# Regrouping the rows of a ReLU row sum into three contiguous blocks of 15, 97 and 16 rows per partition, with a final store of 64 B rows

## The chip, the cores and the metric

One core of a Trainium2 chip. Three of its engines matter here: VectorE and ScalarE compute, and SP issues the DMAs, the transfers between the memory of input and output and the core's own buffers. The trace lists each DMA as packets. When a DMA's data are in place, it has raised its semaphore, a counter that an engine can wait for; that moment is called its landing. The metric is the device time of one execution in microseconds (us), lower is better. A run lists its time and the span of the profiled records, which is about 1.5 us shorter.

## The reference

```python
def setup_inputs():
    batch, seq, dim = 32, 512, 1024
    return {"x": np.random.randn(batch, seq, dim).astype(np.float32)}

def reference(x):
    return np.sum(np.maximum(x, 0), axis=-1).astype(np.float32)
```

The input is 16,384 rows of 1024 floats, 4 KB each, 67.1 MB in all. The output is one float per row, 64 KB. With 128 partitions each partition gets 128 rows.

## The kernel before

Seven chunks of 16 rows per partition go through three buffers, and then a tail of 8, 4, 2 and 1 rows and one last row in two halves. In each chunk but the last, ScalarE applies ReLU and VectorE reduces; in four rows of the sixth chunk, in the last chunk and in the tail both engines do ReLU and sum row by row in one instruction. All loads and stores are issued by SP. Which rows a partition owns is free, since rows are independent. Before, the first 2048 rows form a block of their own (16 neighbouring rows per partition, so partition p starts 64 KB after partition p-1), and all others form a block of 112 rows per partition (a pitch of 448 KB). In the output, each partition's results within a block are contiguous too.

```python
    x0 = xr[0 : P * BIG, :].rearrange("(p j) d -> p j d", p=P)      # block 1: 16 rows per partition
    o0 = of[0 : P * BIG].rearrange("(p j) -> p j", p=P)
    xv = xr[P * BIG :, :].rearrange("(p j) d -> p j d", p=P)        # block 2: 112 rows per partition
    ov = of[P * BIG :].rearrange("(p j) -> p j", p=P)
    # ... cut: buffers and semaphores ...
    for c in range(NBIG + 1):                                       # the chunks
        if c >= NB:
            sp.wait_ge(s_dve, 3 * (c - NB + 1))                     # a buffer is free again
        if c < NBIG:
            sp.dma_start(
                out=buf[:, c % NB, :, :],
                in_=xv[:, (c - 1) * BIG : c * BIG, :] if c else x0[:, :, :],
            ).then_inc(s_in[c], 16)
    # ... cut: loads of the tail (8, 4, 2, 1 rows) ...
    sp.dma_start(                                                   # last row, first half
        out=buf[:, tb, r, 0 : LAST[0]], in_=xv[:, J - BIG - 1, 0 : LAST[0]]
    ).then_inc(s_in[-2], 16)
    sp.dma_start(out=last[:, 0 : LAST[1]], in_=xv[:, J - BIG - 1, LAST[0] : D]).then_inc(
        s_in[-1], 16                                                # last row, second half
    )
    sp.dma_start(out=o0[:, :], in_=res[:, 0:BIG]).then_inc(s_out0, 16)   # early store, 64 B rows
    # ... cut: the work on the chunks and the tail ...
    act.wait_ge(s_in[-2], 16)
    on_act(buf[:, tb, BIG - 1, 0 : LAST[0]], last[:, LAST[1] : LAST[1] + 1]).then_inc(s_tact, 1)
    dve.wait_ge(s_tact, 1)
    dve.wait_ge(s_in[-1], 16)
    on_dve(last[:, :], res[:, J - 1 : J]).then_inc(s_tdve, 1)       # 512 values and ScalarE's sum
    sp.wait_ge(s_tdve, 1)
    sp.dma_start(out=ov[:, :], in_=res[:, BIG:J]).then_inc(s_out, 16)    # final store, 448 B rows
    sp.wait_ge(s_out0, 16)
    sp.wait_ge(s_out, 16)
```

## Time and profile before

| | before |
|---|---|
| time, median of the first 3 runs | 162.49 us (162.36 to 162.69) |
| span of the profiled run | 161.0 us |
| DMA: share of 16 engines' span | 97.1% |
| VectorE, ScalarE busy | 76%, 63% |
| a 64 KB packet repeats on an engine every | 2.414 us, or 434 GB/s on 16 engines |

The page of the kernel before: the DMA rows of the slices (tenths of the engines busy, then GB/s), the queue, and the issues to the output (size in KB, us from issue to landing).

```profile
span 161.0 us, 144 instructions
...
DMA  7979979979979979979979979979979969999992
GB/s 260 521 309 472 521 309 472 521 309 472 521 309 472 521 309 472 521 309 472 521 309 472 521 309 472 521 309 472 521 309 472 521 260 521 391 391 431 413 403 71
...
q1 hardware_dynamic: 2160, 67.18, 97.1%
...
out_dram<-res SPq DMA_DIRECT2D x1, 56.0 KB, 1.6
```

The swing between 309 and 521 GB/s is no stall: the 64 KB packets of the 16 engines start within 0.8 us of each other, every 2.414 us, and a slice of 4.03 us sees sometimes more of these starts and sometimes fewer. The queue is busy from its first load to its last, so the loads set the time. What is left lies before the first packet and after the last one.

The head and the end of the kernel before, from its timeline (start us, us, engine, line, operation, and in brackets the idle time before it and what ended it):

```profile
22.77 14.04 ACT L107 ACTIVATE buf<-buf 128x4096 f32<-128x4096 f32 x3 [20.77 <-DMA buf<-in_x_dram]
...
157.96 0.63 ACT L87 ACTIVATE buf<-buf 128x512 f32<-128x512 f32 x1 [0.81 <-DMA buf<-in_x_dram]
158.44 0.08 DVE L90 DVE_READ_ACCUMULATOR buf<-buf 128x1 f32 x1
158.50 0.19 ACT L87 ACTIVATION_READ_ACCUMULATOR buf<-buf 128x1 f32 x1
158.72 0.69 DVE L90 TENSOR_SCALAR_CACHE_REDUCE last<-last 128x513 f32<-128x513 f32 x1 [0.19 <-ACT buf L87]
159.33 0.08 DVE L90 DVE_READ_ACCUMULATOR last<-last 128x1 f32 x1
159.44 0.34 SPq L140 DMA_DIRECT2D out_dram<-res  x1
```

ScalarE's first activation marks when chunk 0 has landed. At the end, the last VectorE instruction waits for ScalarE's half row. The final store is issued at 159.44, and the span ends 1.6 us later.

### The profile page before, as it was taken

The numbers are of one execution on the slowest core, as the hardware profiler recorded it, in microseconds if no ns is written. First come the engines' busy times: TensorE is split into PE (matmuls) and PEld (weight loads), VectorE is DVE, ScalarE is ACT, GpSimd is POOL, SyncE is SP. The second block draws the span as 40 slices with busy tenths as digits, with TensorE's granted clock in tenths as the row PEclk, the third lists the DMA queues.
The fourth block names the chain that finished last, engine by engine and source line by source line (L and its number), as shares of the span: only waits on it lengthen the run. The fifth ranks groups of instructions, "written<-read, shape, count | busy, mean of one in ns | idle before, by whom it ended". The sixth has DMA issues, their size and how long they took to land.

```text
span 161.0 us, 144 instructions
## 1 busy us (share of the span) xinstructions
DVE 122.0 (76%) x56; ACT 101.0 (63%) x55; POOL 0.2 (0%) x4
## 2 busy tenths in 40 slices
DVE  0000004998969898898969989699899999598995
ACT  3000039991599907997099951999339980596972
POOL 0000000000000000000000000000000000000000
DMA  7979979979979979979979979979979969999992
GB/s 260 521 309 472 521 309 472 521 309 472 521 309 472 521 309 472 521 309 472 521 309 472 521 309 472 521 309 472 521 309 472 521 260 521 391 391 431 413 403 71
DMA packets 2160, 67.18 MB, mean 417 GB/s; under 512 B 496, under 2 KB 496, under 8 KB 880
## 3 DMA queue, kind: packets, MB, share of 16 engines
q1 hardware_dynamic: 2160, 67.18, 97.1%
HBM read 67.11 MB, written 0.07 MB: 417 GB/s over the span
## 4 chain that ended last, share of the span: by engine, by line
DMA 69%; ACT 18%; DVE 10%; SPq 1%; issue 0%
DMA buf<-in_x_dram 69%; ACT buf L107 17%; DVE res L109 9%; SPq L71 1%; ACT buf L87 0%; DVE last L90 0%; SPq L64 0%
## 5 line engine op out<-in xcount | busy, mean ns | idle before, releaser
L109 DVE TENSOR_REDUCE res<-buf 128x4 f32<-128x4096 f32 (+3 forms) x18 | 100.4, 5604 | 34.5 <-ACT buf L107 34.5
L107 ACT ACTIVATE buf<-buf 128x4096 f32<-128x4096 f32 (+3 forms) x18 | 80.9, 4555 | 47.3 <-DMA buf<-in_x_dram 47.3
L87 ACT ACTIVATE buf<-buf 128x1024 f32<-128x1024 f32 (+1 forms) x18 | 18.4, 1024 | 9.7 <-DMA buf<-in_x_dram 9.7
L90 DVE TENSOR_SCALAR_CACHE_REDUCE buf<-buf 128x1024 f32<-128x1024 f32 x18 | 21.0, 1216 | 2.7 <-DMA buf<-in_x_dram 2.5
L87 ACT ACTIVATION_READ_ACCUMULATOR buf<-buf 128x1 f32 x18 | 3.4, 189 | 0.0
L107 ACT ACT_TABLE_LOAD x1 | 1.3, 1283 | 0.7 <-PEq L156 0.7
L90 DVE DVE_READ_ACCUMULATOR buf<-buf 128x1 f32 x18 | 1.5, 83 | 0.0
L90 DVE TENSOR_SCALAR_CACHE_REDUCE last<-last 128x513 f32<-128x513 f32 x1 | 0.7, 689 | 0.2 <-ACT buf L87 0.2
L156 POOL MEMSET const-bfloat16-1.0<- 128x1 bf16 x1 | 0.1, 102 | 0.0
L156 POOL MEMSET const-uint8-127<- 128x1 uint8 x1 | 0.1, 102 | 0.0
L156 POOL MEMSET const-float32-0.0<- 128x1 f32 x1 | 0.1, 99 | 0.2 <-issue 0.2
L156 POOL MEMSET const-float32-1.0<- 128x1 f32 x1 | 0.1, 99 | 0.0
L90 DVE DVE_READ_ACCUMULATOR last<-last 128x1 f32 x1 | 0.1, 84 | 0.0
## 6 DMA issues: line engine op xcount, KB each, us to landing
buf<-in_x_dram SPq DMA_DIRECT2D x1, 4096.0 KB, 26.7
buf<-in_x_dram SPq DMA_DIRECT2D x1, 2048.0 KB, 31.2
buf<-in_x_dram SPq DMA_DIRECT2D x1, 1024.0 KB, 33.2
buf<-in_x_dram SPq DMA_DIRECT2D x1, 512.0 KB, 34.0
buf<-in_x_dram SPq DMA_DIRECT2D x1, 256.0 KB, 34.2
last<-in_x_dram SPq DMA_DIRECT2D x1, 256.0 KB, 34.3
buf<-in_x_dram SPq DMA_DIRECT2D x7, 36.3
out_dram<-res SPq DMA_DIRECT2D x1, 56.0 KB, 1.6
```

The costliest lines, as they stand in the source:

```text
L71: sp.dma_start(out=buf[:, tb, r : r + n, :], in_=xv[:, (NBIG - 1) * BIG + r : (NBIG - 1) * BIG + r + n, :],).then_inc(s_in[NBIG + i], 16)
L87: return act.activation(t, t, AF.Relu, accum_out=acc)
L90: return dve.tensor_scalar(out=t, in0=t, scalar1=0.0, scalar2=None, op0=ALU.max, op1=ALU.add, accum_out=acc)
L107: act.activation(t, t, AF.Relu).then_inc(s_act, 1)
L109: dve.tensor_reduce(out=res[:, c * BIG + r : c * BIG + r + n], in_=t, axis=X, op=ALU.add).then_inc(s_dve, 1)
L156: nc = _bacc.Bacc("TRN2", target_bir_lowering=False, num_devices=1)
```

## The change

Its intent is to shorten the end: if the last 16 rows of each partition are a block of their own, the final store writes 16 results per partition (64 B) in place of 112 (448 B), and the others go out earlier, behind the loads. The remaining 112 rows are cut 15 + 97, so the first chunk needs two loads (15 rows of block 1, one row of block 2), and the pitches between partitions become 60, 388 and 64 KB.

```diff
+REGIONS = [15, 97, 16]
+CHUNKS = [[(0, 0, 15), (1, 0, 1)]] + [[(1, 16 * c + 1, 16)] for c in range(6)]
-    x0 = xr[0 : P * BIG, :].rearrange("(p j) d -> p j d", p=P)
-    o0 = of[0 : P * BIG].rearrange("(p j) -> p j", p=P)
-    xv = xr[P * BIG :, :].rearrange("(p j) d -> p j d", p=P)
-    ov = of[P * BIG :].rearrange("(p j) -> p j", p=P)
+    start = [sum(REGIONS[:i]) for i in range(len(REGIONS))]
+    xv = [
+        xr[P * s : P * (s + n), :].rearrange("(p j) d -> p j d", p=P)
+        for s, n in zip(start, REGIONS)
+    ]
+    ov = [of[P * s : P * (s + n)].rearrange("(p j) -> p j", p=P) for s, n in zip(start, REGIONS)]
 ... cut ...
-            sp.dma_start(
-                out=buf[:, c % NB, :, :],
-                in_=xv[:, (c - 1) * BIG : c * BIG, :] if c else x0[:, :, :],
-            ).then_inc(s_in[c], 16)
+            i = 0
+            for g, j, n in CHUNKS[c]:
+                sp.dma_start(
+                    out=buf[:, c % NB, i : i + n, :], in_=xv[g][:, j : j + n, :]
+                ).then_inc(s_in[c], 16)
+                i += n
 ... cut: the tail is read from xv[-1], waits count the loads of a chunk ...
-    sp.dma_start(out=o0[:, :], in_=res[:, 0:BIG]).then_inc(s_out0, 16)
+    sp.wait_ge(s_fact, 1)          # both engines are done with the last chunk
+    sp.wait_ge(s_fdve, 1)
+    for g in range(len(REGIONS) - 1):
+        sp.dma_start(
+            out=ov[g][:, :], in_=res[:, start[g] : start[g] + REGIONS[g]]
+        ).then_inc(s_store, 16)
 ... cut ...
     sp.wait_ge(s_tdve, 1)
-    sp.dma_start(out=ov[:, :], in_=res[:, BIG:J]).then_inc(s_out, 16)
-    sp.wait_ge(s_out0, 16)
+    sp.dma_start(out=ov[-1][:, :], in_=res[:, start[-1] : J]).then_inc(s_out, 16)
+    sp.wait_ge(s_store, 16 * (len(REGIONS) - 1))
     sp.wait_ge(s_out, 16)
```

More of the change, by code (lines that the diff above doesn't have):

```diff
@@ L6 @@
 BIG = 16
-NBIG = 7
 NTWO = 6
 NB = 3
+REGIONS = [15, 97, 16]
+CHUNKS = [[(0, 0, 15), (1, 0, 1)]] + [[(1, 16 * c + 1, 16)] for c in range(6)]
 STEPS = [4, 5, 7]
@@ L33, in bass_relu_sum_kernel @@
     J = B * S // P
-    assert BIG * NBIG + sum(TAIL) + 1 == J and sum(LAST) == D
+    NBIG = len(CHUNKS)
+    assert BIG * NBIG + sum(TAIL) + 1 == J == sum(REGIONS) and sum(LAST) == D
     xr = x.rearrange("b s d -> (b s) d")
     of = out.rearrange("b s -> (b s)")
-    x0 = xr[0 : P * BIG, :].rearrange("(p j) d -> p j d", p=P)
-    o0 = of[0 : P * BIG].rearrange("(p j) -> p j", p=P)
-    xv = xr[P * BIG :, :].rearrange("(p j) d -> p j d", p=P)
-    ov = of[P * BIG :].rearrange("(p j) -> p j", p=P)
+    start = [sum(REGIONS[:i]) for i in range(len(REGIONS))]
[4 more added lines that the diff above has]
+    ov = [of[P * s : P * (s + n)].rearrange("(p j) -> p j", p=P) for s, n in zip(start, REGIONS)]
     buf = nc.alloc_sbuf_tensor("buf", [P, NB, BIG, D], fp32)
@@ L50, in bass_relu_sum_kernel @@
     s_dve = nc.alloc_semaphore("s_dve")
+    s_fact = nc.alloc_semaphore("s_fact")
+    s_fdve = nc.alloc_semaphore("s_fdve")
     s_tact = nc.alloc_semaphore("s_tact")
     s_tdve = nc.alloc_semaphore("s_tdve")
-    s_out0 = nc.alloc_semaphore("s_out0")
+    s_store = nc.alloc_semaphore("s_store")
     s_out = nc.alloc_semaphore("s_out")
@@ L70, in bass_relu_sum_kernel @@
     for i, n in enumerate(TAIL):
-        sp.dma_start(
-            out=buf[:, tb, r : r + n, :],
-            in_=xv[:, (NBIG - 1) * BIG + r : (NBIG - 1) * BIG + r + n, :],
-        ).then_inc(s_in[NBIG + i], 16)
+        sp.dma_start(out=buf[:, tb, r : r + n, :], in_=xv[-1][:, r : r + n, :]).then_inc(
+            s_in[NBIG + i], 16
+        )
         tail.append((r, n, s_in[NBIG + i]))
         r += n
-    sp.dma_start(
-        out=buf[:, tb, r, 0 : LAST[0]], in_=xv[:, J - BIG - 1, 0 : LAST[0]]
-    ).then_inc(s_in[-2], 16)
-    sp.dma_start(out=last[:, 0 : LAST[1]], in_=xv[:, J - BIG - 1, LAST[0] : D]).then_inc(
+    sp.dma_start(out=buf[:, tb, r, 0 : LAST[0]], in_=xv[-1][:, BIG - 1, 0 : LAST[0]]).then_inc(
+        s_in[-2], 16
+    )
+    sp.dma_start(out=last[:, 0 : LAST[1]], in_=xv[-1][:, BIG - 1, LAST[0] : D]).then_inc(
         s_in[-1], 16
     )
-    sp.dma_start(out=o0[:, :], in_=res[:, 0:BIG]).then_inc(s_out0, 16)
+    sp.wait_ge(s_fact, 1)
[4 more added lines that the diff above has]
+        ).then_inc(s_store, 16)
     def on_act(t, acc):
@@ L98, in bass_relu_sum_kernel @@
         b, steps = c % NB, STEPS if c < NTWO - 1 else MIXED
-        act.wait_ge(s_in[c], 16)
+        act.wait_ge(s_in[c], 16 * len(CHUNKS[c]))
         if steps is MIXED:
-            dve.wait_ge(s_in[c], 16)
+            dve.wait_ge(s_in[c], 16 * len(CHUNKS[c]))
             for i in (BIG - 4, BIG - 3):
@@ L119, in bass_relu_sum_kernel @@
     for c in range(NTWO, NBIG):
-        act.wait_ge(s_in[c], 16)
-        dve.wait_ge(s_in[c], 16)
+        act.wait_ge(s_in[c], 16 * len(CHUNKS[c]))
+        dve.wait_ge(s_in[c], 16 * len(CHUNKS[c]))
         for i in range(BIG):
-            (on_act if i % 2 else on_dve)(*row(c, i))
+            ins = (on_act if i % 2 else on_dve)(*row(c, i))
+            if i >= BIG - 2:
+                ins.then_inc(s_fact if i % 2 else s_fdve, 1)
     for r, n, s in tail:
```

## The prediction

> **What bounds the kernel now.** The load stream. The DMA queue view has it busy for 97.1% of 16 engines' span, and the slices show no hole. In the DMA packet records the loads run for 156.4 us (67.1 MB). Each engine starts a 64 KB packet every 2.414 us, so 16 engines move 434 GB/s. The Trainium skill, "DMA: Bandwidth & Descriptors", section Specifications, names a fabric ceiling of 435 GB/s; the trace agrees, so the steady stream has nothing to gain. VectorE is 76% and ScalarE 63% busy, and SP's waits show that buffers come free early: chunk 3 is issued at 44.5 us behind two queued chunks, the tail's loads at 122 us, 16 us before chunk 6 lands. The engines do not hold up the stream.
>
> Outside it lie a head of 2 us (with first packets of 2.9 to 3.6 us) and an end of 2.6 us (timeline): the last load lands at 158.46, the last VectorE work runs 158.72 to 159.42, the final store is issued at 159.44, its packets run 160.6 to 160.97, and the span ends at 161.04. The unprofiled time is 1.4 us more.
>
> **What the change does.**
>
> 1. The final store shrinks from 128 rows of 448 B to 64 B, on the critical path. Its issue and the 1.2 us to its first packet stay. Its packets take 0.336 us from first to last, some 0.1 of it skew between engines; the rest is 8 packets of 25 ns and one for the semaphore per engine. The old 64 B store's packets were 7 ns apart. Estimate: 8 x (25 - 7) = 0.15 us less.
>
> 2. The other results go in two earlier stores (60 B and 388 B rows), issued when chunk 6 is done at 148.2 us. They queue behind the tail's loads, as the old 64 B store did, take some 0.3 us per engine and end over a microsecond before the final store's first packet. Their issues, 0.4 us each, fall in SP's idle wait of 34.2 us. Worth 0.
>
> 3. The first chunk becomes two loads: 8 more packets and a semaphore packet per engine. A 4 KB packet repeats every 155 ns, a 64 KB one every 2.414 us, which fits 4.4 ns per packet plus a fixed rate: 8 x 4.4 + 6 = 0.04 us more, on the path.
>
> 4. The row pitch between partitions goes from 64 KB (first chunk) and 448 KB (the rest) to 60, 388 and 64 KB. Packets already run at the ceiling; I expect the same rate. The head could move by 0.2 us either way, and the tail's short packets (4 KB in 159 ns, 2 KB in 84 to 96 ns) may slow a little at the 64 KB pitch. I book 0.
>
> Sum: -0.15 + 0.04 = -0.1 us, below 0.1%.
>
> **Predicted time:** 162.35 us, range 161.8 to 162.9. Chances: faster by over 2% 0.01, within 2% 0.98, slower by over 2% 0.01.
>
> **What would show it.** Step 1: final store from issue to landing 1.4 to 1.5 us, not 1.6. Step 2: the early stores land before the final one's first packet. Step 3: 128 packets each of 60 KB and 4 KB, chunk 0 landing within 0.1 us of before. Step 4: 64 KB packets still 2.42 to 2.43 us on average; loads 156.4 us from first to last.
>
> **What would make it wrong.** A pitch that makes packets slow or uneven among engines (loads over 157 us); a faster head from the new addresses; unaligned 60 B and 388 B stores so slow that they delay the last load on a late engine or the final store behind them.

## The result, and the profile after

| | before | after |
|---|---|---|
| time, median of 6 runs each | 162.53 us (162.33 to 162.71) | 162.78 us (162.44 to 163.05) |
| ratio | 1 | 1.0015, 95% interval 1.0000 to 1.0029 |
| span of the profiled run | 161.0 us | 161.3 us |

A ratio is the mean time of one kernel's fast runs over the mean of the other's of the same rounds, so it is not quite the ratio of the medians. The change gained nothing; it may have cost 0.25 us. That is far inside 2%, but its sign is not the predicted one, and the later runs confirmed it: a second timing of the changed kernel gave 1.0030 (1.0018 to 1.0042).

The page of the changed kernel, the same rows as above (the three issues to the output are from its DMA view):

```profile
span 161.3 us, 147 instructions
...
DMA  7999999979979979989989989989989989999992
...
q1 hardware_dynamic: 2448, 67.18, 97.1%
...
out_dram<-res SPq DMA_DIRECT2D x1, 48.5 KB, 10.5
out_dram<-res SPq DMA_DIRECT2D x1, 7.5 KB, 10.1
out_dram<-res SPq DMA_DIRECT2D x1, 8.0 KB, 1.4
```

The final store now takes 1.4 us from issue to landing in place of 1.6. The step that the change was made for works.

The head and the end of the changed kernel, from its timeline:

```profile
23.09 14.04 ACT L120 ACTIVATE buf<-buf 128x4096 f32<-128x4096 f32 x3 [21.08 <-DMA buf<-in_x_dram]
...
158.25 0.63 ACT L100 ACTIVATE buf<-buf 128x512 f32<-128x512 f32 x1 [0.80 <-DMA buf<-in_x_dram]
158.75 0.08 DVE L103 DVE_READ_ACCUMULATOR buf<-buf 128x1 f32 x1
158.79 0.19 ACT L100 ACTIVATION_READ_ACCUMULATOR buf<-buf 128x1 f32 x1
159.17 0.69 DVE L103 TENSOR_SCALAR_CACHE_REDUCE last<-last 128x513 f32<-128x513 f32 x1 [0.34 <-DMA last<-in_x_dram]
159.78 0.08 DVE L103 DVE_READ_ACCUMULATOR last<-last 128x1 f32 x1
159.89 0.33 SPq L155 DMA_DIRECT2D out_dram<-res  x1
```

Two things moved. ScalarE's first activation starts 0.32 us later (23.09 against 22.77), and the loads after it keep that delay. And the last VectorE instruction now waits for its own data: ScalarE was done at 158.98, but the second half row came only at 159.05.

The semaphore records of the trace date every landing to the nanosecond. Each load has 16 increments in the trace, and the time of the sixteenth is its landing (chunk 0 of the changed kernel has two loads, so there it is the thirty-second). All values from the span's start, in us:

```
                                   before    after
chunk 0 landed                     22.750   23.064
chunk 6 landed                    138.870  139.185
  from chunk 0 to chunk 6         116.120  116.121
last row, first half landed       157.940  158.229
last row, second half landed      158.574  159.048
  between the halves                0.634    0.819
last load packet ended            158.103  158.401
```

The stream from chunk 0 to chunk 6 takes the same 116.12 us, although its pitch changed from 448 to 388 KB. The loss sits in the first chunk (0.31 us) and between the two halves of the last row (0.19 us). In that last place the data packets are not late: the last load packet ended 0.30 us later than before, which is the head's delay, but its landing came 0.65 us after it and not 0.47 us.

The prediction's times of packets are on another zero than the timeline: they are 0.36 us late. Its "last load lands at 158.46" is the end of the last load packet, 158.10 us here, and its final store's "160.6 to 160.97" is 160.28 to 160.62 us. From issue to first packet the final store took 0.84 us and not 1.2.

### The profile page after: what moved, and what is told of

The parts are those of the page before. It is cut to its first block, busy times and chain, and to the rows that moved or that the text cites. A ratio compares the mean times of both kernels' runs of the same rounds, so it can differ in the third digit from the quotient of the medians.

```text
span 161.3 us, 147 instructions
## 1 busy us (share of the span) xinstructions
DVE 122.0 (76%) x56; ACT 101.0 (63%) x55; POOL 0.2 (0%) x4
## 4 chain that ended last, share of the span: by engine, by line
DMA 69%; ACT 17%; DVE 10%; SPq 2%; issue 0%; DVEq 0%
DMA buf<-in_x_dram 48%; DMA last<-in_x_dram 21%; ACT buf L120 17%; DVE res L122 9%; SPq L80 1%; SPq L73 1%; DVE last L103 0%; SPq L85 0%; DVEq L150 0%
```

## The experiments

Twelve kernels were run, four at a time on one chip, each in 5 rounds beside the kernel before; the four share its runs. Three theories stood at the start:

- Head theory: the changed first chunk makes the head longer, through its split (two loads) or through its pitch of 60 KB.
- Early-store theory: the two early stores, which stand in the queues behind the last loads, delay the landing of the last load.
- Chance theory: head and tail move by 0.3 us from run to run, whatever the kernel.

The head is measured by one more number from the packet records: when the slowest of the 16 engines ends its first packet. The records do not name the engine, but in the first chunk each engine's packets follow each other without a gap, so the sixteen chains can be told apart by their times. Where the first packet is 60 KB and not 64 KB, 0.15 us is added, the time of the missing 4 KB at the steady rate, so that all can be compared.

The table has all traces, in us. "Halves" is the time between the landings of the two halves of the last row; "4 KB packets" is the mean duration of the tail's 4 KB packets in ns.

| kernel | first packets end: mean, slowest | chunk 0 landed | chunk 6 to 1-row load | halves | 4 KB packets | ratio to before (95%) |
|---|---|---|---|---|---|---|
| before | 5.04, 5.49 | 22.75 | 18.41 | 0.634 | 162 | 1 |
| before_again | 5.05, 5.30 | 22.56 | 18.39 | 0.625 | 162 | 0.9999 (0.9987 to 1.0011) |
| after | 5.20, 5.74 | 23.06 | 18.40 | 0.819 | 162 | 1.0015 (1.0000 to 1.0029) |
| after_again | 5.20, 5.62 | 22.95 | 18.38 | 1.202 | 164 | 1.0030 (1.0018 to 1.0042) |
| split_only | 5.02, 5.42 | 22.85 | 18.38 | 0.623 | 162 | 1.0008 (0.9996 to 1.0021) |
| no_split | 5.05, 5.43 | 22.70 | 18.65 | 0.672 | 199 | 1.0003 (0.9989 to 1.0017) |
| no_split_again | 5.11, 5.35 | 22.64 | 18.39 | 0.662 | 179 | 0.9991 (0.9978 to 1.0003) |
| no_early | 5.20, 5.84 | 23.15 | 18.38 | 0.605 | 162 | 1.0027 (1.0015 to 1.0040) |
| split_later | 5.17, 5.71 | 22.96 | 18.40 | 0.931 | 165 | 1.0030 (1.0017 to 1.0042) |
| two_blocks | 5.04, 5.36 | 22.59 | 18.38 | 0.685 | 167 | 1.0000 (0.9986 to 1.0013) |
| pitch_68 | 5.14, 5.83 | 23.05 | 18.39 | 0.632 | 161 | 1.0028 (1.0015 to 1.0040) |
| shift_4k | 4.97, 5.27 | 22.52 | 18.39 | 0.630 | 161 | 1.0003 (0.9990 to 1.0016) |
| swap_stores | 5.05, 5.25 | 22.52 | 18.67 | 0.854 | 191 | 1.0003 (0.9989 to 1.0016) |
| partial_rows | 5.03, 5.29 | 22.57 | 18.47 | 0.679 | 187 | 0.9995 (0.9982 to 1.0007) |

From chunk 0 to chunk 6 all fourteen traces lie between 116.08 and 116.15 us. Each kernel or repeat has one trace, so the columns are read by groups of traces, and the ratios come from all of a kernel's runs.

### before_again: the kernel before, unchanged

> The kernel before, unchanged: a control for noise, in time and in the trace. Every theory: ratio 1.000, within 0.001. Head theory (the changed first chunk makes the head 0.3 us longer): ScalarE's first activation starts within 0.1 us of 22.77 us, as in the first trace of before. Chance theory (head and tail move by 0.3 us from run to run whatever the kernel): it starts elsewhere by 0.2 us or more, towards the 23.09 us of the changed kernel.

Measured: 162.36 us against 162.44 us, ratio 0.9999. The first activation started at 22.58 us, 0.19 us earlier than in the first trace, so the head does move by 0.2 us by itself, which is more than the head theory had allowed. But it moved away from the changed kernel's 23.09 us. Everything after chunk 0 repeated: from the landing of chunk 0 to the last VectorE work it took 135.92 us (135.97 in the first trace), and from there to the span's end 2.32 us both times.

### after_again: the changed kernel, unchanged

> The changed kernel once more. Head theory: ratio to before 1.0015 to 1.002 again, ScalarE's first activation again at 23.0 to 23.2 us, last VectorE work again at about 159.15 us. Chance theory: ratio between 0.999 and 1.001, first activation anywhere from 22.7 to 23.1 us.

Measured: 162.92 us against 162.44 us, ratio 1.0030, above the expected range of the head theory. The first activation came at 22.97 us (just under the expected 23.0). The last VectorE work came at 159.42 us, later than expected, because the halves were now 1.20 us apart. So the loss is no chance, and it has two parts of which the second varies: 0.16 us in one trace, over 0.5 us in the other. The lines of this kernel's last instruction and of its wait, from the view of that tile:

```profile
L103 DVE TENSOR_SCALAR_CACHE_REDUCE last<-last x1: 690/690/690, 159.4 to 159.4; 128x513 f32<-128x513 f32 x1
...
  DMA last<-in_x_dram: 0.7, 1
```

The second line says that the engine sat idle for 0.7 us until the load of `last` had landed.

### no_split: blocks of 16, 96 and 16 rows

```diff
-REGIONS = [15, 97, 16]
-CHUNKS = [[(0, 0, 15), (1, 0, 1)]] + [[(1, 16 * c + 1, 16)] for c in range(6)]
+REGIONS = [16, 96, 16]
+CHUNKS = [[(0, 0, 16)]] + [[(1, 16 * c, 16)] for c in range(6)]
```

> Blocks of 16, 96 and 16 rows per partition, the first chunk one load of 16 rows: the change without its split and without the 60 KB pitch, with its early stores and its 64 B final store. Head theory: first activation back at about 22.77 us, time 0.3 us below the changed kernel, so 0.999 to 1.000 of before. Early-store theory (the two early stores behind the last loads delay the last landing by 0.16 us): only that much stays, so with the 0.2 us saved by the store the ratio is 0.9995 to 1.0. Chance theory: about 0.999, the store's 0.15 to 0.2 us alone.

Measured: 162.56 us against 162.44 us, ratio 1.0003. The first activation went back to 22.72 us, as the head theory has it, and the halves to 0.67 us. From the last VectorE work to the span's end it took 2.17 us, so the final store's gain is in the trace. But it did not show in the time: the tail from chunk 6 to the one-row load took 18.65 us and not 18.40. The miss is told with the second run of this kernel below.

### split_only: the kernel before with its first chunk loaded in two parts

```diff
-            sp.dma_start(
-                out=buf[:, c % NB, :, :],
-                in_=xv[:, (c - 1) * BIG : c * BIG, :] if c else x0[:, :, :],
-            ).then_inc(s_in[c], 16)
+            i = 0
+            for n in (15, 1) if c == 0 else (BIG,):
+                src = xv[:, (c - 1) * BIG : c * BIG, :] if c else x0[:, i : i + n, :]
+                sp.dma_start(out=buf[:, c % NB, i : i + n, :], in_=src).then_inc(s_in[c], 16)
+                i += n
```

(The first wait of ScalarE counts 32 and not 16.)

> The kernel before with only its first chunk split into loads of 15 rows and 1 row, same addresses, pitch 64 KB, same stores. By my sum of packet overheads: 0.04 us longer, ratio 1.0002, first activation at about 22.81 us. Head theory with the split as the cause: 0.3 us longer, ratio 1.002, first activation at about 23.1 us. Head theory with the 60 KB pitch as the cause: as by my sum.

Measured: 162.60 us against 162.44 us, ratio 1.0008, with an interval that holds both 1.0002 and 1.002. The first activation came at 22.87 us, 0.1 us after the first trace of before and 0.29 us after the second. The first packets ended as early as before (mean 5.02, slowest 5.42), unlike in the changed kernel (5.20; 5.74 and 5.62). So the split alone does not make the slow first packets. From the slowest first packet to the chunk's last semaphore packet this trace took 17.09 us against 16.90 before, 0.19 us where my sum has 0.04; in the two traces of the changed kernel it took 16.94 and 16.95, which is my sum (16.95 in no_early, which has the same split). One trace cannot say more than that the split costs between 0.04 and 0.2 us.

### no_early: the changed kernel without its early stores

```diff
-    for g in range(len(REGIONS) - 1):
-        sp.dma_start(
-            out=ov[g][:, :], in_=res[:, start[g] : start[g] + REGIONS[g]]
-        ).then_inc(s_store, 16)
...
-    sp.wait_ge(s_store, 16 * (len(REGIONS) - 1))
```

The output is wrong.

> The changed kernel without its two early stores; their results are missing, so the output is wrong on purpose. Early-store theory (the unaligned 60 B and 388 B rows, queued behind the last loads, delay the last load's landing): the last half row lands 0.62 to 0.68 us after the first half, as before (0.82 and 1.20 us in the two traces of the changed kernel), the last VectorE work is released by ScalarE and no longer by the load, and the time falls 0.2 to 0.5 us below the changed kernel's. If the landing is late for another reason (chance, or the tail's 64 KB pitch): no change in either.

Measured: the halves went back to 0.605 us, and the last VectorE work was again released by ScalarE:

```profile
L99 DVE TENSOR_SCALAR_CACHE_REDUCE last<-last x1: 690/690/690, 159.1 to 159.1; 128x513 f32<-128x513 f32 x1
...
  ACT buf L96: 0.2, 1
```

From the landing of chunk 0 to the last VectorE work it took 135.91 us, as in the kernel before. But the time did not fall: 162.87 us, ratio 1.0027, where 0.2 to 0.5 us less than the changed kernel had been expected. This run's head was the slowest of all (chunk 0 at 23.15 us, one engine's first packet starting only at 3.39 us), and its final store was issued 0.08 us later after the last VectorE work than in the changed kernel. Together these ate what the tail gave back against the first trace of the changed kernel (spans 161.31 and 161.34 us), but not all of it against the second (161.58 us). For the other four executions there is no trace; all five spans lie at 161.1 to 161.3 us, against 161.1 to 161.4 and 161.2 to 161.6 us in the two timings of the changed kernel. So the traces show that the early stores delay the landing, and the timings do not resolve what it is worth.

### split_later: blocks of 17, 95 and 16 rows

```diff
-REGIONS = [15, 97, 16]
-CHUNKS = [[(0, 0, 15), (1, 0, 1)]] + [[(1, 16 * c + 1, 16)] for c in range(6)]
+REGIONS = [17, 95, 16]
+CHUNKS = [[(0, 0, 16)], [(0, 16, 1), (1, 0, 15)]] + [[(1, 16 * c - 17, 16)] for c in range(2, 7)]
```

> Blocks of 17, 95 and 16 rows: the first chunk is one load of 64 KB packets at a pitch of 68 KB, the second chunk is split 1 + 15, and the early stores have unaligned rows of 68 B and 380 B. Early-store theory: last half row late again, 0.8 us or more after the first half. Pitch theory (first packets are slow where their pitch is not a multiple of 64 KB): mean end of the first packets at about 5.2 us, as in the two traces of the changed kernel, and first activation at 22.9 to 23.0 us. Split theory (the second descriptor set in the first chunk costs it): mean end at 5.04 us and first activation at 22.6 to 22.75 us, as before. Time near the changed kernel by the first two, 0.2 us less by the last.

Measured: 162.90 us, ratio 1.0030. The first chunk is one load of 64 KB packets here, yet the first packets ended late (mean 5.17, slowest 5.71) and chunk 0 landed at 22.96 us. The halves were 0.93 us apart. Both as the pitch and the early-store theories have it; the split is moved to the second chunk, and nothing improved.

### no_split_again: blocks of 16, 96 and 16 rows, a second time

> Blocks of 16, 96 and 16 rows once more, to see whether the first run's 0.3 us slower tail (chunk 6 to last half row 19.99 us against 19.70) was chance. Pitch and early-store theories together: first activation at 22.6 to 22.75 us, last half row 0.62 to 0.68 us after the first half, and chunk 6 to last half row at 19.70 us, so a time 0.15 to 0.2 us below before, ratio 0.999. If the tail's 64 KB pitch or the aligned stores cost it: 19.9 to 20.0 us and ratio 1.000 again.

Measured: 162.25 us against 162.39 us, ratio 0.9991 with an interval up to 1.0003. The head (22.64 us), the halves (0.662 us) and the tail (19.74 us from chunk 6 to the last half row) were as expected. Yet the first run's slow tail was not quite chance. In all four runs with these blocks (this one, no_split, swap_stores and partial_rows) the tail's 4 KB packets took 179 to 199 ns on average, against 161 to 167 ns in the ten other traces, five of which read the same rows in the tail at the same 64 KB pitch, so it is not the tail's own pitch. It cost 0.0 to 0.3 us before the one-row load had landed. What these blocks have that the others lack is not settled; the runs only show that the cost comes with the 16, 96, 16 layout.

### two_blocks: blocks of 112 and 16 rows

```diff
-REGIONS = [15, 97, 16]
-CHUNKS = [[(0, 0, 15), (1, 0, 1)]] + [[(1, 16 * c + 1, 16)] for c in range(6)]
+REGIONS = [112, 16]
+CHUNKS = [[(0, 16 * c, 16)] for c in range(7)]
```

> Two blocks, 112 and 16 rows per partition: one early store of 448 B rows (a multiple of 64 B), the final store of 64 B rows, no split, pitch 448 KB from the first chunk on. Pitch and early-store theories: head and tail as before (first activation 22.6 to 22.75 us, last half row 0.62 to 0.68 us after the first), final store 0.2 us shorter, ratio 0.999. If any early store of 56 KB behind the loads delays the last landing: ratio 1.000 to 1.002 and the last half row 0.8 us or more after the first.

Measured: 162.35 us against 162.39 us, ratio 1.0000. The trace is close to what was expected in every part: chunk 0 at 22.59 us, halves 0.685 us, tail 18.38 us, and from the last VectorE work to the span's end 2.18 us against 2.32 before. Its span, 160.73 us, was the shortest of all traces. The saving of 0.15 us is 0.0009 of the time, and the interval of 0.9986 to 1.0013 neither shows nor excludes it. A 448 B row behind the loads, 56 KB in all, does not delay the landing.

### pitch_68: the kernel before, first chunk read at a pitch of 68 KB

```diff
-    x0 = xr[0 : P * BIG, :].rearrange("(p j) d -> p j d", p=P)
+    x0 = xr[0 : P * (BIG + 1), :].rearrange("(p j) d -> p j d", p=P)[:, 0:BIG, :]
```

The first 2048 results are wrong.

> The kernel before, with one thing changed: its first chunk reads 16 rows per partition at a pitch of 17 rows, 68 KB, instead of 16 (the results of the first 2048 rows are wrong on purpose). No split, stores as before. Pitch theory: mean end of the first packets 5.17 to 5.20 us (5.02 to 5.11 in the five traces at 64 KB and the one at 448 KB), first activation 22.9 to 23.1 us, time 0.2 to 0.35 us above before, ratio 1.001 to 1.002. If the split or the stores were the cause: mean end 5.02 to 5.11 us, ratio 1.000.

Measured: 162.81 us against 162.44 us, ratio 1.0028 (1.0015 to 1.0040), a little more than expected. This one changed line, with no split and the old stores, costs as much as the whole change. Chunk 0 landed at 23.05 us. The mean end of the first packets, 5.14 us, is a little under what I had written, but the slowest, 5.83 us, is among the two latest of all. The first activation in this trace, from its timeline:

```profile
23.07 7.97 ACT L107 ACTIVATE buf<-buf 128x4096 f32<-128x4096 f32 x2 [21.07 <-DMA buf<-in_x_dram]
```

and in the trace of before_again:

```profile
22.58 7.98 ACT L107 ACTIVATE buf<-buf 128x4096 f32<-128x4096 f32 x2 [20.57 <-DMA buf<-in_x_dram]
```

### shift_4k: the kernel before, first chunk read from one row further on

```diff
-    x0 = xr[0 : P * BIG, :].rearrange("(p j) d -> p j d", p=P)
+    x0 = xr[1 : P * BIG + 1, :].rearrange("(p j) d -> p j d", p=P)
```

Wrong as well.

> The kernel before, with its first chunk's load started one row (4 KB) later at the same 64 KB pitch, so that every 64 KB packet crosses a multiple of 64 KB counted from the start of the input (wrong results for the first 2048 rows on purpose). If crossing such a boundary is what makes the first packets slow: mean end 5.17 to 5.20 us, ratio 1.001 to 1.002, as in the run at a pitch of 68 KB. If the pitch itself does it: mean end 5.02 to 5.11 us, ratio 1.000.

Measured: 162.50 us against 162.44 us, ratio 1.0003; chunk 0 landed at 22.52 us and the slowest first packet ended at 5.27 us. So it is not that packets cross multiples of 64 KB, counted from the start of the input (where the input starts in memory is not on record). It is the pitch: at 60 and 68 KB the slowest first packet ended at 5.62 to 5.84 us in five traces, at 64 and 448 KB at 5.25 to 5.49 us in nine. The two groups stay apart on each of the three chips, so it is not the chip. The 60 KB pitch was never run alone, but at a 64 KB pitch the split with its 60 KB packets (split_only) left the first packets as before, and with the early stores taken out (no_early) they stayed slow.

### swap_stores: blocks of 16, 96 and 16 rows, early stores of 60 B and 388 B rows

```diff
... cut: REGIONS and CHUNKS as in no_split ...
-    for g in range(len(REGIONS) - 1):
-        sp.dma_start(
-            out=ov[g][:, :], in_=res[:, start[g] : start[g] + REGIONS[g]]
-        ).then_inc(s_store, 16)
+    for s, n in ((0, 15), (15, 97)):
+        rows = of[P * s : P * (s + n)].rearrange("(p j) -> p j", p=P)
+        sp.dma_start(out=rows, in_=res[:, s : s + n]).then_inc(s_store, 16)
```

The results go to wrong places.

> Blocks of 16, 96 and 16 rows as in the run without the split, but the two early stores write rows of 60 B and 388 B, each block without gaps (wrong places on purpose). Early-store theory: first activation 22.6 to 22.75 us, last half row 0.8 us or more after the first half, last VectorE work released by the load, time 0.2 us or more above the two runs of these blocks with rows of 64 B and 384 B, ratio 1.001. If unaligned rows are not the cause: 0.62 to 0.68 us, ratio 0.9995.

Measured: the halves were 0.854 us apart, against 0.672 and 0.662 with rows of 64 B and 384 B, and the last VectorE work was released by the load after 0.4 us of waiting. The loads are the same, so the rows' shape does it. The time, 162.56 us, ratio 1.0003, equals the slower of the two runs of these blocks with whole rows (1.0003 and 0.9991) and does not resolve it; the 0.2 us more that I had expected did not show in it.

```profile
L102 DVE TENSOR_SCALAR_CACHE_REDUCE last<-last x1: 689/689/689, 159.0 to 159.0; 128x513 f32<-128x513 f32 x1
...
  DMA last<-in_x_dram: 0.4, 1
```

### partial_rows: the same blocks, early stores of 60 B at a pitch of 64 B and of 380 B at 384 B

```diff
... cut: REGIONS and CHUNKS as in no_split ...
-            out=ov[g][:, :], in_=res[:, start[g] : start[g] + REGIONS[g]]
+            out=ov[g][:, 0 : REGIONS[g] - 1], in_=res[:, start[g] : start[g] + REGIONS[g] - 1]
```

256 results are missing.

> Blocks of 16, 96 and 16 rows, but the two early stores leave out the last result of each row: rows of 60 B at a pitch of 64 B and of 380 B at a pitch of 384 B (256 results are missing on purpose). If rows that end inside a 64 B block are enough to delay the last landing: last half row 0.8 us or more after the first. If two rows, written by two engines, must share a 64 B block: 0.62 to 0.68 us, as with whole blocks.

Measured: halves 0.679 us, released by ScalarE, ratio 0.9995.

```profile
L103 DVE TENSOR_SCALAR_CACHE_REDUCE last<-last x1: 690/690/690, 158.6 to 158.6; 128x513 f32<-128x513 f32 x1
...
  ACT buf L100: 0.2, 1
```

Rows of 60 B and 380 B do no harm where each starts at a multiple of 64 B of the output. What does is that rows start off such multiples and so share a 64 B block with their neighbour; this run does not tell these two apart, and no record shows which engine wrote which row. Nor was it shown that the block is one of 64 B: the packed rows of 60, 68, 380 and 388 B are no multiples of 32, 16 or 8 B either. Over all fourteen traces: halves 0.82 to 1.20 us in the four with rows of 60, 68, 380 or 388 B packed without gaps, 0.60 to 0.69 us in the ten others.

## Why the prediction was right or wrong

The time fell within the range, and "within 2%" was right. That the range held owes more to its width than to the sum: the second timing of the changed kernel, 162.92 us, lies just above its upper end of 162.9. The sum of the small terms had the wrong sign: -0.1 us predicted, +0.25 us measured in the first 6 runs and +0.5 us in the second 5.

The two traces of the changed kernel, against the mean of the two of before, add up like this (us):

| term | predicted | after | after_again |
|---|---|---|---|
| start to chunk 0 landed | +0.04 | +0.41 | +0.29 |
| chunk 0 landed to last VectorE work | 0 | +0.16 | +0.53 |
| last VectorE work to the span's end | -0.15 | -0.15 | -0.16 |
| sum | -0.1 | +0.42 | +0.66 |

- What bounds the kernel: right. Chunk 0 to chunk 6 took 116.1 us in every trace, whatever was changed.
- Step 1, the final store: right in mechanism, and in size partly by luck. From the start of the last VectorE work to the span's end it took 2.32 us before and 2.17 and 2.16 us after. But "8 x (25 - 7)" compares the duration of a 448 B packet with the distance between two 64 B packets. By distance the 448 B packets followed each other every 20 to 21 ns, which gives 8 x (21 - 7) = 0.11 us. The store's packets ran 0.33 us from first to last before and 0.21 us after, 0.12 us less; the other 0.03 us came off before and after them.
- Step 2, the early stores: half right. They did land well before the final store's first packet (the last at 159.40 us, against packets from 160.72 us). "Worth 0" failed. Rows packed at 60 and 388 B delay the landing of the last load, which stands ahead of them in the queues, by 0.2 to 0.6 us. The prediction named this only as a risk ("so slow that they delay the last load on a late engine"). The packets themselves were not slow, 11 and 24 ns; it is the increments of the load's semaphore that came late. Next to nothing of it is hidden behind VectorE's wait for ScalarE: counted from chunk 0 the landing came 0.19 and 0.56 us later, and VectorE started 0.16 and 0.53 us later. With its packet times on the wrong zero the prediction had the landing 0.26 us before VectorE's start; it came 0.15 us before it, and in the changed kernel VectorE started 0.12 us after the landing that it waited for, so only some 0.03 us was to spare.
- Step 3, the split: the sum of packets, 0.04 us, agrees with the two traces of the changed kernel. "Chunk 0 landing within 0.1 us of before" failed, mainly for the reason in step 4.
- Step 4, the pitch: this step failed, and with step 2 it makes up the miss. "Packets already run at the ceiling; I expect the same rate" holds for the steady stream, but for the head I wrote "could move by 0.2 us either way" and "I book 0". It moved one way only, later: in the five traces at 60 and 68 KB chunk 0 landed at 22.95 to 23.15 us, in the other nine at 22.52 to 22.85 us. At a pitch of 60 KB in place of 64 KB the slowest first packet ended 0.34 and 0.22 us later than the mean of the two traces of before, most of the head's 0.41 and 0.29 us. The run at 68 KB shows that a changed pitch alone is enough, with a ratio of 1.0028. The loads ran 156.66 us from first packet to last, not the "156.4 us" that step 4 was to show. Why the first packets depend on the pitch and the later ones do not is open.

The Trainium skill's "DMA: Bandwidth & Descriptors", section Specifications, gives 435 GB/s as the fabric ceiling, and this case agrees (434 GB/s on 16 engines in the steady stream). The reading from it was sound for the steady stream, but it says nothing of the first packet.

Left open: what the late landing is worth in time on average, since the run without early stores did not get measurably faster; how an early store delays the increments of a load ahead of it; whether 64 B is the block that counts; and what slows the 4 KB packets in the 16, 96, 16 layout.

## What to carry to other kernels

Here every change of layout left the steady stream as it was and acted at the two ends, so look at the first packets and the last landing one by one, not at the mean rate. Keep small stores that stand behind the last loads in whole 64 B blocks that no two rows share (that did no harm here; a smaller block was not tried), and try the pitch of the first transfer before giving up an even one for a better fit elsewhere. A saving of 0.1% needs its own proof in the trace: from the last VectorE work to the end it took 2.16 to 2.18 us in eight of the nine traces with the 64 B final store (2.25 in no_early) against 2.32 to 2.34 us in the five others, while the timings could not resolve it.

## What the Trainium skill lacked or had wrong

- "DMA: Bandwidth & Descriptors", section "Latency and other measured facts", tells of copies between HBM tensors at row pitches of 512 KiB to 8 MiB, large powers of two, that get slower, and that 4 KiB of padding on the 4 MiB pitch restored the full rate. It has nothing on pitches below, or on loads into the core's buffers. Here a load at a pitch of 64 KB plus 4 KB had slower first packets (slowest ended at 5.83 us against 5.25 to 5.49 us at 64 KB) at an equal steady rate, and cost 0.28% of the time.
- The same page, section "Queues, rings and completion order", says that a semaphore increment lands only after every earlier write from its engine, which no run here tests. No page says that writes queued later can delay it: with packed 60 B and 388 B rows behind it, the last load landed 0.65 and 1.05 us after its last packet had ended, against 0.46 to 0.47 us in the kernel before and 0.42 us without those stores.
- The same page, section Specifications, has a minimum of 512 B for full line rate and says that shorter transfers are done as read-modify-write. Rows of 64, 384 and 448 B are shorter too and did not delay the landing here. No page says what packed rows do that share a block: in the same layout the halves were 0.85 us apart with them and 0.66 to 0.68 us without.
- The same page, section "Where 436 GB/s comes from", says that for transfers between HBM and SBUF (the core's own buffers) the HBM side, about 358 GB/s, binds. Taken alone that sentence misleads: the steady stream of this one-core program moved 434 GB/s. (The page's section "Bandwidth" does limit the figure to both cores of an HBM domain streaming at once.)
